# Two diffusion-transformer layers on one core: eleven local edits of order, in the opening, the attention, both FFNs and the retention

## The chip, the cores and the metric

The kernel runs on one core of a Trainium2 chip. Its engines are called PE (TensorE, matrix products; PEld is its weight load), DVE (VectorE), ACT (ScalarE), POOL (GpSimd) and SP (SyncE, which issues most transfers). The metric is device time in microseconds (us) of one execution. The kernel before took 1732.3 us (median of three runs, 1731.79 to 1732.33).

## The reference

512 latent tokens `x` and 256 context tokens `ctx`, 1024 wide, pass two layers. Layer 0 mixes by windowed grouped-query attention (16 heads of 64, 4 key heads, a sink logit), layer 1 by bidirectional retention (4 heads, 256 wide keys, 512 wide values); each is followed by a SwiGLU FFN of 2816. All products are in float32.

```python
def rms_norm(x, g):
    y = x * lax.rsqrt(jnp.mean(x * x, axis=-1, keepdims=True) + EPS)
    return y * g
def modulate(h, shift, scale):
    return h * (1 + scale) + shift
...
for i in range(DEPTH):
    mx = jnp.split(silu(c) @ ada_w[i] + ada_b[i], 6, axis=-1)        # and mc from c_ctx
    h_x = modulate(rms_norm(x, norm1_g[i]), mx[0], mx[1])            # and h_c
    out_c, out_x = (windowed_gqa_sink if i == 0 else bidir_retention)(h_x, h_c, ...)
    x = x + mx[2] * out_x
    x = x + mx[5] * swiglu(modulate(rms_norm(x, norm2_g[i]), mx[3], mx[4]), ffn_w_in[i], ffn_w_out[i])
    # the context likewise in layer 0
return x
```

The retention's decays are `log_g = log_sigmoid(decay_logit)`, eight numbers.

## The kernel before

Activations lie with the model dimension on the partitions: eight tiles of 128 x 512 for the latent tokens (`res`), four of 128 x 512 for the context (two of 256 tokens in each). A float32 product is made of three products (L148, L149, L150) in a rounded format: a weight or activation is split into a high part (a copy on ACT, `whi`) and the rest (a subtraction on DVE, `wlo`). Weights come through a ring of raw tiles (`wraw`) that SP's queue fills.

**Opening** (to about 80 us). It is written out by hand (`manual_schedule`, from L538): PE, DVE and ACT do what stands there in that order. ACT squares the eight latent tiles, DVE adds them up (`add_square`, L211), PE sums the result over the partitions with a matrix of ones (L543). `busy` (L434) is a product whose result is not used; it stands where PE would have nothing to do. `neg_half_rstd` makes of the sum the norm's factor: a logarithm, an exponential (both L101) and a square (L196) on ACT, and two operations on DVE (L197, L198). `ada_quarter` makes the first 256 shift and scale columns of the adaLN modulation: products L335, a copy of the rows (L353 for the scales, L360 for the shifts), a transpose (L355, L362), two additions (L343, L344) and the column `acol` (L114). `hidden0` applies factor and `acol` (`hs`, L449), adds the shift (ACT, L453) and makes the rest (L457). Then the first key products start (`keys`, L468).

**Attention** (80 to 300 us). Here and below a list scheduler sets each engine's order from the code's order, its dependences and its own costs. 24 blocks of queries are scored in pairs of heads (`score`: PE L756 into one of three banks `S2`, DVE L757 reads the bank, masks it and takes the minimum) and turned (transposes L776, products with values L801). A table `steps` says at which of the half blocks further work is put in: `make_q` projects the next two query heads (L148 to L150), squares them (L660), applies gain and rotation, and `norms` sums the squares (L685). `decays` at step 13 works out the retention's decay columns, 1 + 1 operations on ACT and 21 small ones on DVE (L856 to L870).

**FFN of layer 0** (300 to 865 us). `first_two` and `context_shape` make sums of tiles that stand for a two-by-two block product with seven products (`seven`, L989). The adaLN columns of layer 1 come in beside it on DVE: 48 tiles of 128 x 1024, loaded by POOL's queue into one buffer `adaw` (L269) and multiplied with the condition row (L272), once or twice each. `ada_next` takes the next of them and puts it behind the operation that it is given. `last_output` makes the FFN's last sums by halves of tokens (products into banks `pj` and `Z`, added by L1209) and the squares for the next norm.

**Retention** (865 to 1385 us). One head after the other: queries and keys (`whi` L1316, `wlo` L1317, products L1399), values, state, then the gate: `gated` multiplies norm and gate, and `values_first` starts the next head.

**FFN of layer 1** (1385 to 1728 us): `first_two` and `seven` again, with the output's sums (L254) between them.

Of the kernel before, what the change touches and what calls it, by code (L numbers as in the profile page):

```python
# [12 lines left out]
ALU = mybir.AluOpType  # L13
# [36 lines left out]
def dit_kernel(ctx, tc, xT, cT, crow, small, consts, masks, tabs0, tabs1, jtab, adaQ, adaN, adaT, wst, out):  # L50
# [272 lines left out]
    def ada_quarter_load(q):  # L323
        w = [T(st_p, 1024, "adan", 8) for _ in range(4)]
        for i in (2, 3, 0, 1):
            nc.sync.dma_start(w[i], adaQ[q, i // 2, i % 2])
        return w
# [73 lines left out]
    res0[1] = load_stream(1, 0, 4)  # L401
    wq.append(ada_quarter_load(1))
# [135 lines left out]
    with tc.manual_schedule(engines={mybir.EngineType.PE, mybir.EngineType.DVE, mybir.EngineType.Activation}):  # L538
        squares0(0, *range(KT))
        for k in range(4):  # L540
            busy(SX, k)
        tot = kvv[1]
        nc.tensor.matmul(tot, ones, ssq[0], start=True, stop=True)  # L543

        def first_fill():
# [60 lines left out]
        end = ada_unit(UNITS[1], wu[1])  # L606
        rope_key(kn[0])
        keys(1, 2)
        key_factor(0)
# [34 lines left out]
    def make_q(j, w=None, raw=None, behind=()):  # L644
# [11 lines left out]
        def shape(s):  # L656
            n = NTOK[s]
            sq, qn = t_sq(n), t_hn(n)
            nc.scalar.activation(qn, o[s], AF.Identity, scale=qk_gain[:, 0:1])
            q_done.append(nc.scalar.activation(sq, o[s], AF.Square))  # L660
# [19 lines left out]
        def norms():  # L680
            tot = pj(12)
# [169 lines left out]
    def decays(behind):  # L851

        dec = sm_t[:, C_DEC:C_DEC + 8]
        after(nc.scalar.activation(t1, dec, AF.Abs), behind)
        lnexp(t1, t1, AF.Exp, scale=-1.0)
        nc.vector.tensor_scalar(t2, t1, 2.0, None, op0=add)  # L856
        nc.vector.reciprocal(t2, t2)
        nc.vector.tensor_tensor(t1, t1, t2, op=mult)
        nc.vector.tensor_tensor(t2, t1, t1, op=mult)
        NTERM = 10  # L860
        nc.vector.tensor_scalar(t3, t2, 1.0 / (2 * NTERM + 1), None, op0=mult)
        for k in range(NTERM - 1, 0, -1):
            nc.vector.scalar_tensor_tensor(t3, t3, 1.0 / (2 * k + 1), t2, add, mult)
        nc.vector.scalar_tensor_tensor(t3, t3, 1.0, t1, add, mult)
        nc.vector.tensor_scalar(t1, dec, 0.0, None, op0=ALU.min)
        nc.vector.scalar_tensor_tensor(lg, t3, -2.0, t1, mult, add)
        nc.vector.tensor_scalar(dcol[:, 0, :], lg[:, 0:4], 128.0, None, op0=mult)
        nc.vector.tensor_scalar(dcol[:, 1, :], lg[:, 4:8], 640.0, None, op0=mult)
        nc.vector.tensor_scalar(dcol[:, 2, :], lg[:, 4:8], 384.0, None, op0=mult)
        nc.vector.tensor_scalar(dcol[:, 3, :], lg[:, 4:8], -1.0, None, op0=mult)  # L870
# [63 lines left out]
    steps.setdefault(13, []).append(lambda: decays([blocks[6].scored]))  # L934
    steps[34].append(lambda: split_o(0))
    steps[35] = [lambda: split_o(1), weight]
# [56 lines left out]
    def quarter_sums(g, u):  # L993

        l_, r_ = slice(0, 512), slice(512, 1024)
        nc.vector.tensor_tensor(g[:, l_], u[:, l_], g[:, l_], op=sub)
        nc.vector.tensor_tensor(u[:, l_], u[:, r_], u[:, l_], op=sub)
        nc.vector.tensor_tensor(u[:, r_], u[:, r_], g[:, l_], op=sub)
        nc.vector.tensor_tensor(g[:, r_], g[:, r_], u[:, r_], op=sub)  # L999
# [42 lines left out]
    def token_sums():  # L1042

        h1, h2 = THIRDS
        for k in range(4):
            t1, t2 = tm[k], tm[k + 4]
            nc.vector.tensor_tensor(t2[:, h2], t1[:, h2], t2[:, h2], op=add)
            nc.vector.tensor_tensor(t1[:, h2], t1[:, h1], t1[:, h2], op=sub)
            nc.vector.tensor_tensor(t1[:, h1], t2[:, h2], t1[:, h1], op=sub)
            nc.vector.tensor_tensor(park[:, k * 384:(k + 1) * 384], t2[:, h1], t1[:, h1], op=sub)  # L1050
# [63 lines left out]
    last_product, copies, rounded = [None], [], [None]  # L1114

    def seven(middle=None):
# [3 lines left out]
        split(g, *b11)  # L1120
# [4 lines left out]
        nc.vector.tensor_tensor(g[:, r_], g[:, r_], g[:, l_], op=sub)  # L1125
# [8 lines left out]
        if cr:  # L1134
            ada_next(half)
# [15 lines left out]
        nc.scalar.copy(c22, Y)  # L1151
# [52 lines left out]
    def last_output(acts):  # L1204
# [8 lines left out]
        for s, res, c, part in ((0, xr, HALVES[0], HALVES[0]), (1, cres, slice(SX, WIDE), slice(0, SC)),  # L1213
                                (0, xr, HALVES[1], HALVES[1])):
            for d in range(KT):
# [14 lines left out]
                sum_up(s, d, o, res, part, s == 1 or c.start == 0)  # L1230
                if s and d == 2:
# [14 lines left out]
    ada_q = []  # L1246
# [13 lines left out]
    for gsz in FFN_GROUPS:  # L1260
        acts = []
        for i in range(gsz):
# [4 lines left out]
            else:  # L1267
                a, end = seven(last_sum if f == PLAIN else None)
                acts.append(a)
                if f == PLAIN:  # L1270
                    ends.pop(0)()
                    cr = cond_rows(fp)
                if i or f == PLAIN + 2:
                    ada_next(end)
# [4 lines left out]
    assert not ada_q  # L1279
# [188 lines left out]
    for hd in range(RH):  # L1468
# [74 lines left out]
        for e, o in halves(Y2):  # L1543
            nc.vector.tensor_tensor(qt[e][:, HALVES[0]], qt[e][:, HALVES[0]], o, op=add)
# [10 lines left out]
        for i in range(2):  # L1555
# [4 lines left out]
            nc.vector.tensor_tensor(v11[i], g12[i], v11[i], op=add)  # L1560
            w2.append(split_chunk(v11[i]))
        parted = last_split[:]
        w3 = [split_chunk(g12[0])]
# [137 lines left out]
        product_v(Zg, quarter_of(4), w22, False, (1,))  # L1701
        for t in range(2):
# [337 lines left out]
```

## Time and profile before

| | |
|---|---|
| median of three runs | 1732.3 us (1731.79 to 1732.33) |
| the profiled execution | 1730.06 us, span 1728.3 us, granted clock 0.999 |
| PE busy | 1706.5 us, 99% of the span |
| DVE, ACT, POOL busy | 1336.0, 841.4 and 120.9 us |
| bytes read from HBM | 201.75 MB, 118 GB/s over the span |

A row of the timeline gives the start in us from the first instruction, the length, the engine, the line of the kernel, the operation, output and input tiles with their shapes, and in brackets the idle time before it with what ended it. A row of the waits gives the engine and line that waited, what for, the us in total, how often, and the longest. A row of a stretch gives its ends and length, the busy time and count of PE, PEld, DVE, ACT and POOL, then PE's granted clock, the share of the transfer engines and GB/s.

### The profile page before, as it was taken

The page shows a single profiled execution, that of the slowest core. Times are in us where ns is not written, and L with a number is a line of the kernel's source. Part 1 is how long each engine was busy: PE and PEld are TensorE (multiplying, and loading weights), DVE is VectorE, ACT ScalarE, POOL GpSimd, SP SyncE. Part 2 cuts the span into 40 slices and gives each one's busy share as a digit, 9 for nine tenths or more (in the row PEclk, how much of TensorE's full clock was granted, in tenths as well). Part 3 has the DMA queues.
Part 4 walks back from the last instruction along what each step waited for, and adds up shares of the span by engine and source line. Part 5 has one row for each costly group of instructions (what it writes and reads, how often), then busy time and mean ns, then how long its engine had stood idle before and what let it go on. Part 6 is the DMA issues. An engine that isn't in the chain of part 4 may idle for free.

```text
span 1728.3 us, 28150 instructions
## 1 busy us (share of the span) xinstructions
PE 1706.5 (99%) x11090; PEld 1535.7 (89%) x11090; DVE 1336.0 (77%) x2377; ACT 841.4 (49%) x1509; POOL 120.9 (7%) x266
## 2 busy tenths in 40 slices
PE   8999999999999999999999999999999999999999
PEld 5888887899999999999998798898898999999998
DVE  6888696488778777787899858758768898778774
ACT  5667696264434233342565624524525555445442
POOL 0033443000000000000000000000000100000000
PEclk9999999999999999999999999999999999999999
DMA  9500014233243434343423534433433333233322
GB/s 374 226 26 26 13 58 163 74 122 111 95 136 129 141 111 158 110 147 110 147 100 122 183 99 131 160 110 118 157 106 112 98 98 122 74 122 99 107 77 86
DMA packets 61908, 205.67 MB, mean 119 GB/s; under 512 B 6864, under 2 KB 7760, under 8 KB 61648
## 3 DMA queue, kind: packets, MB, share of 16 engines
q1 hardware_dynamic: 54864, 178.71, 30.6%
q0 software_dynamic: 6912, 25.17, 4.5%
q8 instruction: 87, 1.43, 0.3%
q14 instruction: 45, 0.37, 0.1%
HBM read 201.75 MB, written 2.10 MB: 118 GB/s over the span
## 4 chain that ended last, share of the span: by engine, by line
PE 40%; DVE 7%; DMA 2%; ACT 1%; issue 1%; SPq 0%; ACTq 0%; DVEq 0%
PE Y L989 6%; PE Z L1399 6%; PE Y L1386 3%; PE Z L989 3%; PE pj L148 2%; PE pj L150 2%; PE pj L149 2%; PE pj L1399 2%; PE X L1386 1%; PE X L989 1%; DMA wraw<-in_wst_dram 1%; DVE wlo L1317 1%; PE X L1399 1%; PE X L148 1%; PE X L150 1%
## 5 line engine op out<-in xcount | busy, mean ns | idle before, releaser
L989 PE MATMUL Y<-aq,whi 128*128 128x384 f32 x640 | 173.7, 335 | 1.1 <-ACT hn L1140 0.7
L254 DVE SCALAR_TENSOR_TENSOR res<-pj,mod,res 128x512 f32<-128x512 f32 (+1 forms) x102 | 74.5, 731 | 68.7 <-PE pj L150 68.3
L989 PEld LDWEIGHTS Y<-aq,whi 128*128 128x128 f32 x640 | 116.6, 188 | 2.1 <-ACT hn L1140 1.4
L140 ACT CAST whi<-wraw 128x1024 fp32r<-128x1024 f32 x75 | 78.7, 1049 | 72.1 <-DMA wraw<-in_wst_dram 25.2
L141 DVE TENSOR_TENSOR wlo<-wraw,whi 128x1024 fp32r<-128x1024 f32 x75 | 91.7, 1223 | 28.5 <-ACT whi L140 27.7
L989 PE MATMUL Y<-aq,wlo 128*128 128x384 f32 x320 | 107.2, 335 | 0.5 <-DVE wlo L166 0.4
L272 DVE CUSTOM_DVE_ANT_0 y<-adaw,crow,small_sb 128x1024 bf16<-128x1024 f32 x64 | 81.9, 1280 | 23.1 <-DMA adaw<-in_adaT_dram 23.1
L1316 ACT CAST whi<-wraw 128x1024 fp32r<-128x1024 f32 x55 | 57.6, 1049 | 72.3 <-PE Y L150 52.3
L101 ACT ACTIVATE pr<-pr,stat,qs 128x513 f32<-128x513 f32 (+2 forms) x96 | 74.1, 775 | 19.1 <-DVE stat L763 17.7
L1399 PE MATMUL Z<-whi,sA 128*128 128x512 f32 x256 | 80.7, 391 | 0.6 <-ACT whi L1316 0.6
L1317 DVE TENSOR_TENSOR wlo<-wraw,whi 128x1024 fp32r<-128x1024 f32 x55 | 67.0, 1223 | 16.4 <-ACT whi L1316 16.3
L165 ACT CAST whi<-wraw 128x1024 fp32r<-128x1024 f32 x40 | 42.0, 1051 | 73.8 <-PE Z L150 43.3
L770 POOL TENSOR_SCALAR pr<-pr,stat 128x512 f32<-128x512 f32 (+2 forms) x96 | 66.5, 706 | 86.5 <-DVE stat L767 67.4
L148 PE MATMUL pj<-ax,whi 128*128 128x512 f32 x176 | 68.9, 392 | 0.7 <-DVE res L254 0.7
L150 PE MATMUL pj<-ax,whi 128*128 128x512 f32 x176 | 68.7, 390 | 0.0
L149 PE MATMUL pj<-ax,wlo 128*128 128x512 f32 x176 | 68.6, 389 | 0.0
L269 POOL DMA_DIRECT2D adaw<-in_adaT_dram x48 | 25.6, 533 | 512.6 <-DVE mod L272 420.7
L989 PEld LDWEIGHTS Y<-aq,wlo 128*128 128x128 f32 x320 | 60.1, 188 | 1.1 <-DVE wlo L166 1.1
L757 DVE CUSTOM_DVE_ANT_0 pr<-S,mask,qs 128x256 f32<-128x256 f32 (+1 forms) x96 | 52.7, 567 | 10.7 <-PE S L756 8.5
L148 PE MATMUL pj<-act,whi 128*128 128x512 f32 (+1 forms) x156 | 60.1, 385 | 0.6 <-DVE res L1209 0.6
L989 PE MATMUL Y<-sA,whi 128*128 128x256 f32 x304 | 60.1, 280 | 0.2 <-ACT res L1842 0.2
L1835 ACT CAST whi<-wraw 128x1024 fp32r<-128x1024 f32 x38 | 39.2, 1052 | 43.1 <-DVE wraw L999 21.6
(620 smaller groups left out, 5613.2 us busy)
## 6 DMA issues: line engine op xcount, KB each, us to landing
wraw<-in_wst_dram SPq DMA_DIRECT2D x231, 512.0 KB, 3.6
adaw<-in_adaT_dram POOLq DMA_DIRECT2D x48, 512.0 KB, 3.8
wx<-in_wst_dram SPq DMA_DIRECT2D x28, 512.0 KB, 4.4
adan<-in_adaQ_dram SPq DMA_DIRECT2D x16, 512.0 KB, 7.3
adan<-in_adaN_dram SPq DMA_DIRECT2D x16, 512.0 KB, 8.0
res<-in_xT_dram SPq DMA_DIRECT2D x16, 256.0 KB, 5.4
q<-in_adaN_dram SPq DMA_DIRECT2D x16, 256.0 KB, 3.7
aq<-in_adaN_dram SPq DMA_DIRECT2D x12, 256.0 KB, 5.3
```

Source lines behind the costliest of these rows:

```text
L101: ins = nc.scalar.activation(*args, **kw)
L140: after(nc.scalar.copy(hi, raw), behind)
L141: after(nc.vector.tensor_tensor(lo, raw, hi, op=sub), low)
L148: after(nc.tensor.matmul(o, whi, xhi, start=first, stop=False), behind)
L149: nc.tensor.matmul(o, wlo, xhi, start=False, stop=False)
L150: return nc.tensor.matmul(o, whi, xlo, start=False, stop=last)
L254: return nc.vector.scalar_tensor_tensor(res[d], o, mods[l, s][:, part, d:d + 1], res[d], mult, add)
L272: after(nc.vector.tensor_tensor_reduce(junk, w, cr[:, s * 1024:(s + 1) * 1024], 1.0, sm_t[:, C_ADAB + l * 48 + j:C_ADAB + l * 48 + j + 1], ...
L989: ins = nc.tensor.matmul(o, p, r, start=first and k + i == 0, stop=k == 3 and i == 2, skip_group_check=not first)
L1317: last_split[0] = nc.vector.tensor_tensor(lo, raw, hi, op=sub)
L1386: ins = nc.tensor.matmul(o[:, e * SC:(e + 1) * SC], p[:, ws], r, start=first and k + e + i == 0, stop=k == 3 and i == 2, skip_group_check= ...
L1399: ins = nc.tensor.matmul(o, p, r, start=first and k + i == 0, stop=k == 3 and i == 2, skip_group_check=not first)
```

## The change

Eleven edits, in the order of the program:

1. Opening: the squares of the seventh latent tile are no longer added by DVE; PE adds them into the sum by a product of its own. Sum and factor are made in two halves of 256 tokens, each step for both halves. Six `busy` products instead of four stand ahead of it. The factor is emitted ahead of `ada_quarter` and no longer between its two products. The shift columns come behind the second `hs` instead of the first.
2. Two context transfers go out between the second and third transfer of the second adaLN quarter instead of ahead of it.
3. The second adaLN unit's products stand behind `keys(1, 2)`.
4. `make_q`: for context queries the square goes ahead of the gain copy; the first head pair's sums go into the bank `pO`.
5. `decays`: one operation per step from step 12 on, instead of all at step 13.
6. `context_shape`: ACT adds the shift to latent columns 384 to 512 only; the sums of tiles add it for columns 0 to 384.
7. `seven` of layer 0: from the second group on the copy of a weight waits for the last copy of the group before.
8. The adaLN tiles of layer 1 in other places: one in the weight's preparation, one behind each adaLN end, the rest in `last_output` behind its second sum.
9. Retention, first head: the last query sums behind the first split of values, and the splits behind the second sum.
10. Retention, end of heads 1 to 3: the gate's additions with the next value weights' splits between them, then `values_first`, then the four `gated`.
11. FFN of layer 1: the order of weight copies, sums and products is tied to the copy of the first product and to the multiplication of the group before.

```diff
-        squares0(0, *range(KT))
-        for k in range(4):
+        opening_sq = lambda n: T(st_p, 512, "hs", 3)[:, :n]
+        for k in range(KT - 2):
+            add_square(0, k, res0[0][k], tmp=opening_sq)
             busy(SX, k)
-        tot = kvv[1]
-        nc.tensor.matmul(tot, ones, ssq[0], start=True, stop=True)
+        y0, z0, tail = ssq[0], t_sq(SX), [opening_sq(SX) for _ in range(2)]
+        tot = [t[:, 0:SC] for t in kvv[0:2]]
+        nc.scalar.activation(tail[0], res0[0][KT - 2], AF.Square)
+        for o, c in zip(tot, HALVES):
+            nc.tensor.matmul(o, ones, tail[0][:, c], start=True, stop=False)
+        for o, c in zip(tot, HALVES):
+            nc.scalar.activation(tail[1][:, c], res0[0][KT - 1][:, c], AF.Square)
+            nc.vector.tensor_tensor(y0[:, c], y0[:, c], tail[1][:, c], op=add)
+            nc.tensor.matmul(o, ones, y0[:, c], start=False, stop=True)
...
+        for step in range(4):
+            for o, c in zip(tot, HALVES):
+                first_factor(step, o, c)
...
-        c0, c1 = ada_quarter(0, wq[0], nc.vector.tensor_copy, lambda: None, first_fill,
-                             lambda: neg_half_rstd(ssq[0], t_sq(SX), tot, D))
+        c0, c1 = ada_quarter(0, wq[0], nc.vector.tensor_copy, lambda: None, first_fill)
         busy(SX)
-        hidden0(0, 0, 1, between=(lambda: low(0, quarters[0]), lambda: low(1, quarters[0])), shifts=c0)
+        hidden0(0, 0, 1, between=(lambda: low(0, quarters[0]), lambda: low(1, quarters[0])), shifts=c0, at=1)
...
-            tot = pj(12)
+            tot = pj(12) if j else pO()[:, 0:12]
...
-    steps.setdefault(13, []).append(lambda: decays([blocks[6].scored]))
+    for i, op in enumerate(decays()):
+        steps.setdefault(12 + i, []).append(lambda i=i, op=op: after(op(), [blocks[12 + i >> 1].scored]))
...
-            for s, c in ((0, slice(0, SX)), (1, slice(SX, WIDE))):
+            for s, c in ((0, slice(384, SX)), (1, slice(SX, WIDE))):
...
+        if waiting:
+            waiting.clear()
+            ada_next(last)
...
-        if cr:
-            ada_next(half)
...
+                while ada_q and not s and d == 1:
+                    ada_next(added[1])
...
+        for ins in [] if hd else late:
+            after(ins, parted)
...
-        gated(2)
-        gated(3)
         if last:
+            gated(2)
+            gated(3)
...
-            b11, Yv, vt, ins = values_first(first_weights_v(hd + 1))
+            b11, Yv, vt, ins = values_first(next_v)
+            for n in (2, 3, 0, 1):
+                gated(n)
...
-        split(u[:, 512:1024], *b22)
-        quarter_sums(g, u)
+        after(nc.scalar.copy(b22[0], u[:, 512:1024]), p1s if f == 5 else [])
+        nc.vector.tensor_tensor(b22[1], u[:, 512:1024], b22[0], op=sub)
+        sums = quarter_sums(g, u)
+        if added:
+            after(sums[0], muls[-1:])
+            after(sums[1], added[:1])
```

How the edits move instructions is seen at three places. The rows name line, operation, output and input tiles, width, and a count of equal rows; lines are those of each kernel. The first is DVE in the opening, from the additions of squares (`y_245`) to the first two modulated tiles (`hs`). Before:

```order
L211 TENSOR_TENSOR y_245<-y_245,sq 128x512 x7
L353 COPY rows<-pT 128x128
L343 TENSOR_TENSOR mod_74<-pT,small_sb 128x2
L344 TENSOR_TENSOR mod_74<-pT,mod_74 128x2
L114 SCALAR_TENSOR_TENSOR acol_78<-mod_74,gm_85 128x2
L197 SCALAR_TENSOR_TENSOR sq<-kvv,sq 128x512
L198 SCALAR_TENSOR_TENSOR y_245<-sq,y_245 128x512
L449 SCALAR_TENSOR_TENSOR hs<-res,acol_78,y_245 128x512
L343 TENSOR_TENSOR mod_74<-pT,small_sb 128x2
L344 TENSOR_TENSOR mod_74<-pT,mod_74 128x2
L449 SCALAR_TENSOR_TENSOR hs<-res,acol_78,y_245 128x512
```

The same stretch of DVE after the change (L562 and L563 are the factor's two operations, L355 the copy of the scale rows, L345 and L346 the additions of columns, L450 the modulated tile):

```order
L211 TENSOR_TENSOR y_245<-y_245,hs 128x512 x5
L551 TENSOR_TENSOR y_245<-y_245,hs 128x256 x2
L562 SCALAR_TENSOR_TENSOR sq<-kvv,sq 128x256
L563 SCALAR_TENSOR_TENSOR y_245<-sq,y_245 128x256
L562 SCALAR_TENSOR_TENSOR sq<-kvv,sq 128x256
L563 SCALAR_TENSOR_TENSOR y_245<-sq,y_245 128x256
L355 COPY rows<-pT 128x128
L345 TENSOR_TENSOR mod_74<-pT,small_sb 128x2
L346 TENSOR_TENSOR mod_74<-pT,mod_74 128x2
L114 SCALAR_TENSOR_TENSOR acol_78<-mod_74,gm_85 128x2
L450 SCALAR_TENSOR_TENSOR hs<-res,acol_78,y_245 128x512 x2
```

The copy of the scale rows with its additions and `acol` stood ahead of the factor's operations and now stands behind them, and both `hs` now stand ahead of the shift's additions. The second place is PE at the start, from the `busy` products to the transpose of the scale rows. Before:

```order
L434 MATMUL kvv<-res,ones_sb 128x512 x4
L543 MATMUL kvv<-y_245,ones_sb 128x512
L335 MATMUL pT<-adan,ccol 32x128 x16
L355 MATMUL pT<-const_sb,rows 128x128
L335 MATMUL pT<-adan,ccol 32x128 x16
```

The same stretch of PE after the change (L548 adds the seventh tile's squares, L552 the other ones'):

```order
L435 MATMUL kvv<-res,ones_sb 128x512 x6
L548 MATMUL kvv<-hs,ones_sb 128x256 x2
L552 MATMUL kvv<-y_245,ones_sb 128x256 x2
L337 MATMUL pT<-adan,ccol 32x128 x16
L357 MATMUL pT<-const_sb,rows 128x128
L337 MATMUL pT<-adan,ccol 32x128 x16
```

Two more `busy` products and four half-width products stand where one full-width product stood. The third place is PE in the attention around 165 us of the trace before, behind the query heads' sums of squares: scores (`S_...`, one name for each bank turn), transposes (`pT`) and query projections (`pj`). Before:

```order
L756 MATMUL S_2259<-kc,q 128x256 x2
L756 MATMUL S_2263<-k,q 128x384 x2
L756 MATMUL S_2269<-kc,q 128x256 x2
L776 MATMUL pT<-const_sb,pr 128x128 x8
L756 MATMUL S_2273<-k,q 128x384
L685 MATMUL pj<-const_sb,sq 128x2 x2
L756 MATMUL S_2273<-k,q 128x384
L148 MATMUL pj<-h,whi 128x512
L756 MATMUL S_2300<-kc,q 128x256 x2
```

The same stretch of PE after the change (L783 are the scores, L803 the transposes, L712 the sums of squares); it ends with the second projection product of eleven that stand ahead of the next score product, `S_2265`:

```order
L783 MATMUL S_2251<-kc,q 128x256 x2
L783 MATMUL S_2255<-k,q 128x384 x2
L803 MATMUL pT<-const_sb,pr 128x128 x3
L783 MATMUL S_2261<-kc,q 128x256 x2
L803 MATMUL pT<-const_sb,pr 128x128 x5
L712 MATMUL pj<-const_sb,sq 128x2 x2
L148 MATMUL pj<-h,whi 128x512
L149 MATMUL pj<-h,wlo 128x512
```

The fourth score of the group came right behind the transposes; now eleven projection products stand between the transposes and it.

More of the change, by code (lines that the diff above doesn't have):

```diff
@@ L658, in shape @@
             sq, qn = t_sq(n), t_hn(n)
+            square = lambda: q_done.append(nc.scalar.activation(sq, o[s], AF.Square))
+            if s:
+                square()
             nc.scalar.activation(qn, o[s], AF.Identity, scale=qk_gain[:, 0:1])
-            q_done.append(nc.scalar.activation(sq, o[s], AF.Square))
+            if not s:
+                square()
             sqs.append(sq)
@@ L1119, in seven @@
         b11 = w_parts(fp, 1)
-        split(g, *b11)
+        after(nc.scalar.copy(b11[0], g), copied_up if f == PLAIN + 1 else [])
+        nc.vector.tensor_tensor(b11[1], g, b11[0], op=sub)
         t1 = T(fp, 512, "bhi", 1, F32R), T(fp, 512, "blo", 1, F32R)
@@ L1150, in seven @@
         product(Y, operand[3], b3, 0, False)
-        nc.scalar.copy(c22, Y)
+        copied_up[:] = [nc.scalar.copy(c22, Y)]
         nc.vector.tensor_tensor(c22, c22, c21, op=add)
@@ L1841, in seven @@
         product(Y, operand_a("11"), b11, 0, True)
-        nc.scalar.copy(p1, Y)
+        p1s[:] = [nc.scalar.copy(p1, Y)]
         product(Z, operand_a(1), b14, 0, True)
```

93 lines of the change are left out of this document (53 added, 40 removed).

## The prediction

> **What bounds the kernel now.** I read the busy times first, then the waits of TensorE (PE), then busy time by stretch, then single rows where PE stands. The busy times say which engine a microsecond has to be taken from (the second line is a group of transfers: issuer, count, size, us from issue to landing; it is needed further below):
>
> ```profile
> PE 1706.5 (99%) x11090; PEld 1535.7 (89%) x11090; DVE 1336.0 (77%) x2377; ACT 841.4 (49%) x1509; POOL 120.9 (7%) x266
> ...
> adaw<-in_adaT_dram POOLq DMA_DIRECT2D x48, 512.0 KB, 3.8
> ```
>
> The span is 1728.3 us and PE is busy for 1706.5 of it. The diff leaves PE's products as they are, so all that it can win is PE's idle time, some 22 us, and time at a lower clock. The waits of PE (engine, line, what it waited for, us in total, times, longest) name the idle time:
>
> ```profile
> PE kvv L434 <- DMA res<-in_xT_dram: 4.1, 1, 4.1
> PE S L756 <- DVE stat L757: 2.8, 2, 2.2
> PE kvv L543 <- DVE y L211: 1.8, 1, 1.8
> PE pj L468 <- ACT h L453: 1.6, 2, 1.0
> PE Y L989 <- ACT hn L1140: 0.7, 1, 0.7
> PE pj L148 <- DVE res L254: 0.7, 1, 0.7
> PE Z L1399 <- ACT whi L1316: 0.6, 1, 0.6
> PE Z L1399 <- DVE wlo L1317: 0.6, 1, 0.6
> PE pj L148 <- DVE res L1209: 0.6, 1, 0.6
> PE pj L685 <- ACT sq L660: 0.5, 1, 0.5
> PE Y L989 <- DVE wlo L166: 0.4, 1, 0.4
> PE X L148 <- ACT sq L107: 0.4, 1, 0.4
> PE Y L989 <- ACT sq L1151: 0.4, 1, 0.4
> PE pj L148 <- DVE qs L688: 0.3, 1, 0.3
> ```
>
> The first row is the wait for the first input and no edit touches it. Nearly every other row has an edit of its own in the diff, so the change is a list of small repairs, each worth at most its row. The stretches (length, PE, PEld, DVE, ACT, POOL busy, granted clock, DMA share, GB/s) show where nothing is left:
>
> ```profile
> 157.00:165.00 8.00, 6.00 (x49) 5.50 (x48) 7.84 (x20) 5.88 (x12) 2.29 (x4) 1.00 0.09 20
> 165.00:172.00 7.00, 6.75 (x34) 5.78 (x35) 6.69 (x25) 3.57 (x11) 2.04 (x4) 0.76 0.14 53
> 1000.00:1380.00 380.00, 379.88 (x2096) 331.33 (x2095) 282.72 (x397) 168.95 (x257) 4.40 (x9) 1.00 0.37 122
> ```
>
> From 1000 to 1380 us PE idles 0.12 us: heads 2 to 4 of the retention have nothing to give. The stretch 165 to 172 is the only one after the start with a clock below 1.00.
>
> **Decays (steps 12 to 35).** The rows around the longest wait (start, length, engine, line, operation, in brackets the idle time before it):
>
> ```profile
> 149.62 0.17 DVE L856 TENSOR_SCALAR lg_t<-lg_t 128x8 f32<-128x8 f32 x1
> ...
> 156.13 0.16 DVE L870 TENSOR_SCALAR dcol<-lg 128x4 f32<-128x4 f32 x1
> ...
> 162.02 1.21 DVE L141 TENSOR_TENSOR wlo<-wraw,whi 128x1024 fp32r<-128x1024 f32 x1
> ...
> 163.27 0.68 DVE L675 TENSOR_TENSOR q<-hn,q 64x512 fp32r<-64x512 f32 x1
> ...
> 165.25 0.45 PE L756 MATMUL S<-k,q 128*128 128x384 f32 x1 [2.25 <-DVE stat L757]
> ```
>
> VectorE (DVE) runs 21 such small operations from 149.62 to 156.13, about 21 x 0.17 = 3.6 us, and from 157 to 165 it is busy 7.84 of 8 us: it is behind, and PE waits 2.25 us for a score bank that it has not read. Right after that the clock is at 0.76 of full speed over 7 us, which costs 7 x 0.24 = 1.7 us. Spread over 24 steps, at most three or four of the 21 stand ahead of that point, so DVE arrives some 3 us earlier, more than the wait. The new PE order speaks for it too: eleven products of 512 columns stand ahead of the score product that waited, where there were none. I take the whole: **-3.9** (2.2 + 1.7). Bounds: 0, if another late DVE operation takes the place, and -4.5 with the second wait of that row (2.8 in all).
>
> [...]
>
> **Other waits, with one answer each.** The attention queries (square before the gain copy, the first sum in another bank): rows 0.5 and 0.3; two scalar operations swap, nothing is added; **-0.6**, between 0 and -0.8. The first part of the FFN (the shift no longer added by ACT over 384 latent columns; c22's copy ahead of the next weight's): rows 0.4 (L107) and 0.4 (L1151); ACT loses eight operations, DVE adds twelve with a scalar in place of plain ones, hidden by DVE's idle time (it is busy 77% of the span); **-0.7**, between +0.3 and -0.8. The adaLN tiles of layer 1 (DVE) in other places: rows 0.7 (L1140) and 0.4 (L166); **-0.9**, between +0.5 and -1.1. First retention head: rows 0.6 (L1316) and 0.6 (L1317); **-1.0**, between 0 and -1.2. In the later heads the gate's additions and next splits now stand ahead of the norm's multiplies, but `values_first` of the next head keeps PE busy behind them; nothing. FFN of layer 1: row 0.7 (L254); **-0.7**, between 0 and -0.8.
>
> **Last output of layer 0's FFN.** The rows there before:
>
> ```profile
> 848.79 1.28 DVE L272 CUSTOM_DVE_ANT_0 y<-adaw,crow,small_sb 128x1024 bf16<-128x1024 f32 x1 [0.92 <-DMA adaw<-in_adaT_dram]
> 850.01 0.48 DVE L1209 SCALAR_TENSOR_TENSOR res<-pj,mod,res 128x256 f32<-128x256 f32 x1
> 850.40 1.27 DVE L272 CUSTOM_DVE_ANT_0 y<-adaw,crow,small_sb 128x1024 bf16<-128x1024 f32 x1
> ...
> 850.88 0.28 PE L150 MATMUL pj<-act,whi 128*128 128x256 f32 x1
> 851.00 0.28 PE L148 MATMUL pj<-act,whi 128*128 128x256 f32 x1
> ```
>
> One tile's two products stood here, the second behind the first sum. Now the first sums come sooner, but one tile more falls in this stage, and there is one buffer: the last tile's transfer of 3.8 us starts when the tile before it has been read. Four sums stand between them, each of which PE takes 12 products at 0.12 us from start to start, about 1.4 us, to feed, so the transfer mostly lies beside 5.6 us of PE's work. The 0.6 may go, or come back three sums later: **0**, between -0.6 and +2.0 (two products more of 1.28 on DVE, less what the banks cover).
>
> **The opening.** This is the one step that I expect to lose. Rows before:
>
> ```profile
> 4.08 6.70 PE L434 MATMUL kvv<-res,ones_sb 128*128 128x512 f32 x8 [4.08 <-DMA res<-in_xT_dram]
> 9.42 3.08 DVE L211 TENSOR_TENSOR y<-y,sq 128x512 f32<-128x512 f32 x4 [0.35 <-ACT sq L210]
> 12.55 1.12 PE L543 MATMUL kvv<-y,ones_sb 128*128 128x512 f32 x2 [1.77 <-DVE y L211]
> 14.76 0.29 DVE L353 COPY rows<-pT 128x128 f32<-128x128 f32 x1 [2.26 <-PE pT L335]
> 15.86 0.16 DVE L114 SCALAR_TENSOR_TENSOR acol<-mod,gm 128x2 f32<-128x2 f32 x1
> 16.57 0.70 PE L434 MATMUL kvv<-res,ones_sb 128*128 128x256 f32 x2
> 16.66 0.69 DVE L198 SCALAR_TENSOR_TENSOR y<-sq,y 128x512 f32<-128x512 f32 x1
> 17.39 0.75 DVE L449 SCALAR_TENSOR_TENSOR hs<-res,acol,y 128x512 f32<-128x512 f32 x1
> 19.21 0.74 PE L468 MATMUL pj<-h,whi 128*128 128x512 f32 x2 [0.97 <-ACT h L453]
> ```
>
> The path to the first key product is squares, sum, factor, modulated input. PE was late by 1.77 us for the sum (12.55), since DVE added squares until 12.50. Now two more products of 512 that only keep PE busy stand ahead of it. An instruction of such a product shows as two rows (four as 8): 4 more rows, at 0.84 (6.70 / 8) or, warm, 0.56 (1.12 / 2). They end at about 4.08 + 6.70 + 2.2 = 13.0, or 12.3 if the warm pitch comes a little earlier. Behind them stand four products of 256 columns, 8 rows of 0.35 (0.70 / 2): the first half's sum ends at 12.3 + 6 x 0.35 = 14.4, the second's at 15.1, where the whole sum ended at 13.67. DVE's shorter chain is so lost behind PE. ACT and DVE then work in halves, which overlap: behind the sum the factor took 17.35 - 13.67 = 3.7 us, and by halves some 3.0 from the second sum, about 18.1 to 18.4, **+0.8 to +1.1**.
>
> Then the order on DVE: the copy of the scale rows (L353) with the transpose, two additions and `acol` behind it took 14.76 to 16.02 and lay beside ACT's work on the factor. They now stand behind all four factor operations, so that their 1.26 us come after y: the first `hs` starts at 18.2 + 1.3 = 19.5 where it was 17.39, **+2.1**. The shift columns now wait for the second `hs` as well, **+0.75**. First keys at 19.21 + 2.85, about 22.1: **+2.9**. PE has from there no slack until 80 us. Bounds: +1.4 (half factors quicker, shift columns no later) and +4.5 (PE idles some 2.6 us for the late copy, and the 2.25 us gap above was followed by a window at half speed, 1.7). The context rows' later loads (needed after the first keys, which move too) and the second unit behind `keys(1, 2)`: nothing, they are covered by PE's products.
>
> **Sum.** -3.9 - 0.6 - 0.7 - 0.9 - 1.0 - 0.7 + 0 + 2.9 = -4.9. The profiled execution took 1730.06 (span 1728.3 and 1.8 around it), 2.2 below the median of 1732.3; against the median the sum gives **1727.4**. About 0.2%, 3.5 us, is what a measurement of this kernel tells from no change: 1728.8 to 1735.8 is "same".
>
> **Rivals.**
> - The opening gains as its halves suggest: if PE's clock is up earlier and DVE's copy finds its rows while it waits anyway, the 1.8 us wait of L543 goes and the order costs nothing: 1732.3 - 7.8 - 1.8 = 1722.7. For it: DVE's additions are shorter by a whole row. Against it: DVE runs in order, and its new order has the copy last. Chance 0.10.
> - The freed DVE time is given back in the attention stage: the score bank's wait appears at another query group. 1727.4 + 3.9 = 1731.3. For it: DVE's run of a weight split (1.2 us) and four query operations without reading a score is still there at each query group. Chance 0.20.
> - The small repairs bring new waits of the same size, so that only decays and opening count: 1732.3 - 3.9 + 2.9 = 1731.3. For it: these are 0.2 to 0.7 us each, and every one is a swap in an order. Chance 0.15.
> - Slower, by one mechanism in the attention stage: the new scheduling makes score waits as long as the one at 165.25 at three places. Each costs 2.2 + 1.7 (the clock falls after it): 1731.3 + 2 x 3.9 = 1739.1 with the decays' gain lost and two beside it. It decides from the point where PE has less ready work than DVE's run lasts, 1.2 + 4 x 0.5 + 0.7 = 3.9 us (L141; four like L675, two of them half as wide; a copy); PE's new order has eleven products of 512 columns and some transposes there, at twice the 0.12 us of the 256-column rows above about 3 us. So the margin is thin; it is slower than before from the second such place (1735.2). Chance 0.10.
>
> **How the numbers follow.** My forecast has 0.45. It lies 1.4 us within "faster" and its terms scatter by 2 to 3 us, so 0.30 of the 0.45 is faster and 0.15 same; the first rival is all faster (0.10); the second and third (0.35) are same but for 0.08, which is faster, and 0.02 slower; the slower rival adds 0.10, of which 0.04 stays within 0.2%. Faster 0.48, same 0.44, slower 0.08. With the bounds of the opening and of the last output, the range goes from 1721.5 (the first rival) to 1735 (the second mishap in the attention).
>
> **What the profile after will show.** Decays: no PE wait above 1 us at 150 to 180 us and no stretch below clock 1.00. Opening: the first key product near 22, the scale rows' copy behind both factor halves, PE idle about 2.6 us ahead of it. The waits of L1140, L166, L1316, L1317, L254 and L107 gone from PE's list. I am wrong if the first keys start before 20 us, if a score wait of over 2 us stands elsewhere, or if PE waits at 845 to 860 us by more than 1 us.

## The result, and the profile after

The changed kernel took 1755.79 us (median of four runs, 1753.18 to 1758.21) against 1732.05 for the kernel before on the same chip: 1.0139 times the time, with a 95% interval of 1.0122 to 1.0157. It is 24 us slower; the forecast was 5 us faster, and no rival priced it so high. The profiled execution took 1753.18, its span is 1751.4 us. The line of busy times:

```profile
PE 1714.3 (98%) x11100; PEld 1540.1 (88%) x11100; DVE 1333.6 (76%) x2379; ACT 839.2 (48%) x1513; POOL 122.8 (7%) x266
```

DVE and ACT do no more work than before (1336.0 and 841.4 us), so the time is not work that was added. PE idles 37.1 us of the span (21.8 before), and its products are busy 7.8 us longer. The waits of PE in the changed kernel:

```profile
PE Y L1011 <- DVE wlo L166: 9.1, 8, 2.3
PE kvv L435 <- DMA res<-in_xT_dram: 4.2, 1, 4.2
PE pT L357 <- DVE rows L355: 2.4, 1, 2.4
PE pj L150 <- DVE act L1095: 2.1, 1, 2.1
PE pj L148 <- ACT act L1094: 1.6, 1, 1.6
PE X L1428 <- DVE wlo L1346: 1.4, 2, 1.1
PE Y L1415 <- DVE wlo L1346: 1.3, 1, 1.3
PE Y L1011 <- ACT res L1884: 1.3, 1, 1.3
...
PE pT L932 <- DMA q<-in_adaN_dram: 1.1, 1, 1.1
...
PE pj L149 <- DVE wlo L141: 0.9, 1, 0.9
```

The waits for the scores at 165 us, for the queries (L685) and for L254 are gone or short. A new one leads the list: the seven-product stage (L1011, before L989) waits eight times for the low part of a weight (`wlo`, L166), 9.1 us in all. Marks in the two traces say where the 23 us of span come from. The first key product starts at 21.20 (before 19.21), the last score of the attention at 298.47 (297.81), the group of seven products that resumes at 522.98 before resumes at 522.67; then the same marks of the next groups are at 621.02 (614.68), 717.64 (706.77) and 812.93 (800.34), and the first retention product at 900.66 (880.78). So most of the loss, 20 us, lies between 523 and 900 us, in the FFN of layer 0: there PE idles 16.1 us (2.0 before), and its granted clock is 0.99 (1.00 before). Another 2.5 us stand behind it, at 900 to 1000 us, where PE's waits sum to 3.9 us (1.4 before). Two stretches there (490 to 530 is an output stage, 530 to 590 the seven-product stage behind it), before:

```profile
490.00:530.00 40.00, 40.00 (x232) 36.15 (x231) 29.68 (x45) 9.37 (x13) 2.11 (x4) 1.00 0.37 120
530.00:590.00 60.00, 60.00 (x347) 58.96 (x346) 49.08 (x74) 25.54 (x43) 3.70 (x7) 1.00 0.46 148
```

and after:

```profile
490.00:530.00 40.00, 40.00 (x233) 36.19 (x232) 23.29 (x35) 8.43 (x11) 0.00 (x0) 1.00 0.21 66
530.00:590.00 60.00, 55.73 (x306) 54.41 (x305) 49.86 (x77) 25.65 (x43) 5.28 (x10) 0.97 0.47 153
```

In the output stage DVE has lost 6.4 us of work (29.68 to 23.29) and POOL issues no transfer, and in the stage behind it PE idles 4.3 us of 60, at a clock of 0.97. What went missing are the adaLN tiles. DVE's waits at 500 to 870 us for their transfers, before and after:

```profile
DVE y L272 <- DMA adaw<-in_adaT_dram: 18.8, 12, 3.8
```

```profile
DVE y L272 <- DMA adaw<-in_adaT_dram: 35.9, 34, 3.6
```

Twelve waits have become 34. DVE's order shows why; here T is a product of an adaLN tile (L272) and o a sum of the output stage (L254), from the first product on, before and after:

```
before  TTTTTToooToToooTooooTooooToTTTTTTTTTToooTooooTo
after   TTTTTTooooooooooooooooTTTTTTTTTTTTTTToooooooooo
```

Before, five products (of four tiles) stood between the sums of an output stage, where DVE waits for PE anyway (8.6 us of the 40 at 490 to 530 us, for products of L150). Now none does, and some fourteen products stand in one run in the seven-product stage. The rows of DVE around the first output stage of the changed kernel:

```profile
486.57 1.28 DVE L272 CUSTOM_DVE_ANT_0 y<-adaw,crow,small_sb 128x1024 bf16<-128x1024 f32 x1 [3.64 <-DMA adaw<-in_adaT_dram]
...
525.88 0.56 DVE L1095 TENSOR_TENSOR act<-sq,act 128x384 fp32r<-128x384 f32 x1 [2.52 <-ACT act L1094]
526.36 1.28 DVE L272 CUSTOM_DVE_ANT_0 y<-adaw,crow,small_sb 128x1024 bf16<-128x1024 f32 x1
...
572.24 1.29 DVE L272 CUSTOM_DVE_ANT_0 y<-adaw,crow,small_sb 128x1024 bf16<-128x1024 f32 x1 [1.29 <-DMA adaw<-in_adaT_dram]
...
574.39 1.22 DVE L166 TENSOR_TENSOR wlo<-wraw,whi 128x1024 fp32r<-128x1024 f32 x1
```

No tile for 40 us, then one right behind L1095, which is the `end` of the group's first seven products (the last operation that `seven` returns; the "adaLN end" of the change's list is this one). Edit 8 ties a tile to that `end`, and in the code it stands ahead of `output(prev)`. PE does the output stage before those products are finished. There is one buffer `adaw`, and it is given out in the order of the code: the tile that waits for the late `end` holds it, and the output's own four tiles queue behind. POOL's rows show the buffer held: it issues a transfer at 488.16, and the next one 42 us later, released by DVE's product:

```profile
488.16 0.53 POOL L269 DMA_DIRECT2D adaw<-in_adaT_dram  x1 [6.00 <-DVE mod L272]
530.28 0.53 POOL L269 DMA_DIRECT2D adaw<-in_adaT_dram  x1 [41.59 <-DVE mod L272]
```

In the kernel before it issues four in that time. Here the four tiles come when the stage that had room for them is over. At 572.24 the second effect shows: DVE stands 1.29 us for a transfer, and the split of the next weight (574.39) stands behind it in DVE's queue. PE gets that weight 2.35 us late:

```profile
575.66 0.45 PE L1011 MATMUL Y<-aq,wlo 128*128 128x384 f32 x1 [2.35 <-DVE wlo L166]
```

### The profile page after: what moved, and what is told of

Read it like the earlier page. It is cut to its first block, busy times and chain, and to the rows that moved or that the text cites. A ratio compares the mean times of both kernels' runs of the same rounds, so it can differ in the third digit from the quotient of the medians.

```text
span 1751.4 us, 28141 instructions
## 1 busy us (share of the span) xinstructions
PE 1714.3 (98%) x11100; PEld 1540.1 (88%) x11100; DVE 1333.6 (76%) x2379; ACT 839.2 (48%) x1513; POOL 122.8 (7%) x266
## 4 chain that ended last, share of the span: by engine, by line
PE 41%; DVE 6%; DMA 1%; ACT 1%; issue 1%; POOL 0%; ACTq 0%; DVEq 0%; SPq 0%
PE Z L1428 6%; PE Y L1011 6%; PE Y L1415 3%; PE Z L1011 3%; PE pj L148 2%; PE pj L150 2%; PE pj L149 2%; PE pj L1428 2%; PE X L1415 1%; PE X L1011 1%; DMA wraw<-in_wst_dram 1%; PE X L150 1%; PE X L1428 1%; PE Y L149 1%; PE X L149 1%; PE Y L150 1%
## 5 line engine op out<-in xcount | busy, mean ns | idle before, releaser
L1011 PE MATMUL Y<-aq,whi 128*128 128x384 f32 x640 | 174.2, 336 | 2.5 <-ACT hn L1173 1.2
L254 DVE SCALAR_TENSOR_TENSOR res<-pj,mod,res 128x512 f32<-128x512 f32 (+1 forms) x102 | 74.4, 730 | 64.4 <-PE pj L150 64.2
L1011 PEld LDWEIGHTS Y<-aq,whi 128*128 128x128 f32 x640 | 116.9, 188 | 3.9 <-ACT hn L1166 1.6
L1011 PE MATMUL Y<-aq,wlo 128*128 128x384 f32 x320 | 108.2, 338 | 9.7 <-DVE wlo L166 9.1
L272 DVE CUSTOM_DVE_ANT_0 y<-adaw,crow,small_sb 128x1024 bf16<-128x1024 f32 x64 | 82.1, 1283 | 40.4 <-DMA adaw<-in_adaT_dram 40.4
L140 ACT CAST whi<-wraw 128x1024 fp32r<-128x1024 f32 x75 | 78.6, 1048 | 70.7 <-PE Z L150 24.7
L1345 ACT CAST whi<-wraw 128x1024 fp32r<-128x1024 f32 x55 | 57.5, 1050 | 75.6 <-PE Y L150 52.9
L1011 PEld LDWEIGHTS Y<-aq,wlo 128*128 128x128 f32 x320 | 60.2, 188 | 12.5 <-DVE wlo L166 11.6
L150 PE MATMUL pj<-ax,whi 128*128 128x512 f32 x176 | 68.7, 390 | 0.0
L1011 PE MATMUL Y<-sA,whi 128*128 128x256 f32 x304 | 60.0, 280 | 1.3 <-ACT res L1884 1.3
L149 PE MATMUL pj<-act,wlo 128*128 128x512 f32 (+1 forms) x156 | 60.1, 385 | 0.9 <-DVE wlo L141 0.9
L1877 ACT CAST whi<-wraw 128x1024 fp32r<-128x1024 f32 x38 | 39.3, 1052 | 44.8 <-DVE wraw L1021 23.6
L148 PE MATMUL pj<-act,whi 128*128 128x512 f32 (+1 forms) x156 | 60.1, 385 | 0.0
L150 PE MATMUL pj<-act,whi 128*128 128x512 f32 (+1 forms) x156 | 59.5, 382 | 0.0
```

Source lines behind the costliest of these rows:

```text
L140: after(nc.scalar.copy(hi, raw), behind)
L148: after(nc.tensor.matmul(o, whi, xhi, start=first, stop=False), behind)
L149: nc.tensor.matmul(o, wlo, xhi, start=False, stop=False)
L150: return nc.tensor.matmul(o, whi, xlo, start=False, stop=last)
L254: return nc.vector.scalar_tensor_tensor(res[d], o, mods[l, s][:, part, d:d + 1], res[d], mult, add)
L272: after(nc.vector.tensor_tensor_reduce(junk, w, cr[:, s * 1024:(s + 1) * 1024], 1.0, sm_t[:, C_ADAB + l * 48 + j:C_ADAB + l * 48 + j + 1], ...
```

## Experiments

The kernel before ran beside them on the same chips: 1730.68 us in the first four, 1730.86 in the next, 1730.09 in the last. Ratios are to it, with their 95% interval; as it moved by up to 2 us between sessions (1732.05 beside the changed kernel), runs of different sessions are compared by their ratios.

**All but edit 8.** Its lines are put back to those of before.

```diff
-        if waiting:
-            waiting.clear()
-            ada_next(last)
...
+        if cr:
+            ada_next(half)
...
-                while ada_q and not s and d == 1:
-                    ada_next(added[1])
...
-                if f > PLAIN:
-                    ada_next(end)
-                if i or f == PLAIN + 2:
-                    waiting.append(f)
+                if i or f == PLAIN + 2:
+                    ada_next(end)
```

> All edits but the adaLN tiles' (edit 8 undone). From the traces the changed kernel loses 20 us between the first group of seven products and the first retention product (-0.3 us at 523 us, +19.9 at 900 us). If edit 8 is the whole of that: 1755.8 - 20 = 1736, so 3 to 4 us above the kernel before, from the opening (+2), the first retention head and the last FFN. If the loss comes from the other edits in this stage (the shift's place, the copy tied to the group before): still about 1755.

Measured: 1729.04 us, ratio 0.9992 (0.9983 to 1.0002). Edit 8 is the whole loss: 1.0139 less 0.9992 is 25 us (27 between the medians). The 1736 that I expected was too high, as I counted only the 20 us up to the first retention product; the waits behind it go as well (at 900 to 1000 us 1.6 us are left of 3.9). The other ten edits together make no difference that this measurement shows.

**Edit 8 alone** on the kernel before, the same lines the other way round.

> The kernel before with edit 8 alone. If edit 8 makes the loss by itself: 1732 + 18 to 20 = 1750 to 1752. If it needs the other edits (a DVE that they already make late): under 1740.

Measured: 1756.06, ratio 1.015 (1.0134 to 1.0165). It makes the loss by itself, 25 us, some 4 us more than I expected; nothing else in the change is needed for it.

**Which part of edit 8.** First, the tile at the group's first `end` is moved into the preparation of the next weight, all else as changed:

```diff
-                if f > PLAIN:
-                    ada_next(end)
                 if i or f == PLAIN + 2:
+                    ada_next(end)
+                if f > PLAIN:
                     waiting.append(f)
```

> The changed kernel, but the tile that stands behind the first adaLN end of each group goes into the next weight's preparation instead; eleven tiles a group as before, and the place ahead of the weight's split is kept (and used once more). Theory 1: that one tile holds the only buffer until the group's first end, which comes after the output stage, so that the output's four tiles come late and fourteen products stand back to back behind 4 us transfers, ahead of weight splits; without it 1736 to 1738. Theory 2: a product ahead of the split b24 delays that split by itself; then 1752 to 1758, as there is one more of them.

Measured: 1728.6, ratio 0.9993 (0.9984 to 1.0002). One tile for each group, tied to another instruction, takes the whole loss away (theory 1, again some 8 us below its number). In its trace the stretch behind the output stage has PE at 60.00 of 60 us again, and of PE's waits at 500 to 900 us two short ones are left:

```profile
490.00:530.00 40.00, 40.00 (x233) 36.14 (x232) 30.10 (x46) 9.53 (x13) 2.11 (x4) 1.00 0.40 124
530.00:590.00 60.00, 60.00 (x347) 58.91 (x346) 49.05 (x74) 25.95 (x43) 3.70 (x7) 1.00 0.44 146
```

```profile
PE Y L1011 <- ACT hn L1166: 0.6, 1, 0.6
PE Y L1011 <- DVE wlo L166: 0.4, 1, 0.4
```

Then the other half of the edit: the tile in the preparation goes behind the split again, the first `end` keeps its tile.

```diff
-        if waiting:
-            waiting.clear()
-            ada_next(last)
         b24 = w_parts(fp, 1)
...
         nc.vector.tensor_tensor(b3[1], u, b3[0], op=sub)
+        if waiting:
+            waiting.clear()
+            ada_next(half)
```

> The other half: the first end of a group keeps its tile, but the product in the preparation stands behind the split b24 again, as before the change. Theory 1: 1752 to 1756, nothing won, since the tiles still fall back to back. Theory 2: 1737 to 1740.

Measured: 1751.58, ratio 1.0122 (1.0107 to 1.0137), 3 us under the whole change by the ratios, whose intervals overlap, and slightly below what theory 1 gave. The rival mechanism (a product ahead of a split) is so at most a small part, and only while the tiles come in a run: in the run before, with the product ahead of the split at more places, it cost nothing that shows. A second buffer for the tiles, which would take the hold away and leave the places, was not tried.

**Transfer or products.** Is it the wait for transfers that makes DVE late, or the products' own time? The transfers of 47 tiles are left out; each product is held behind the one before, so that the order of T and o stays that of the change.

```diff
-            w = T(room, 1024, "adaw", 1 if l else 3)
-        (nc.gpsimd if l else nc.sync).dma_start(w, adaT[l, j])
+            w = (held[:1] or [T(room, 1024, "adaw", 1 if l else 3)])[0]
+        if not held:
+            (nc.gpsimd if l else nc.sync).dma_start(w, adaT[l, j])
```

> The changed kernel with all products of the adaLN tiles of layer 1 in their places and order (each held behind the one before), but only the first of the 48 tiles is loaded and all products use it: 47 transfers of 512 KB are left out. Theory (the loss is DVE standing ahead of weight splits until a transfer into the single buffer lands): DVE's waits for these transfers (35.9 us at 500 to 870 us) go, and the loss with them, 1733 to 1738. Rival (fourteen products of 1.28 us in one stretch are too much work for DVE beside the splits, whatever the transfers do): 1748 or more.

Measured: 1743.26, ratio 1.0073 (1.0058 to 1.0088), between the two. By the ratios some 11 us of the 25 are gone and 14 remain; PE idles 10.3 us at 500 to 900 us, where it was 16.1 in the changed kernel and 0.8 without edit 8. Without waits for transfers the postponed products all become due at the end of the output stage, and run closely:

```profile
527.13 1.28 DVE L277 CUSTOM_DVE_ANT_0 y<-adaw,crow,small_sb 128x1024 bf16<-128x1024 f32 x1
...
529.47 1.28 DVE L277 CUSTOM_DVE_ANT_0 y<-adaw,crow,small_sb 128x1024 bf16<-128x1024 f32 x1
...
531.14 1.28 DVE L277 CUSTOM_DVE_ANT_0 y<-adaw,crow,small_sb 128x1024 bf16<-128x1024 f32 x1
```

and PE at 500 to 900 us waits for the splits that stand behind them (the second row is ACT's copy of a weight, late by the same chain: at 544.32 us ACT has waited 2.33 us for a sum of DVE):

```profile
PE Z L1019 <- DVE blo L166: 3.7, 3, 1.2
PE Y L1019 <- ACT whi L165: 3.1, 4, 1.8
```

So my theory had the cause right (the postponed tiles) and only half of the way: both the transfers and the products' own 1.28 us make DVE late once they come in a run.

**The opening.** On top of edit 8 undone, the halves (edit 1) are undone as well.

> Edit 8 and the opening's halves (edit 1) undone, all else as changed. Theory (the scale rows' copy behind the factor delays the start): the first key product goes from 20.3 to about 19.1 us and the time falls by 1.2 to 2.0 from 1729.0, to 1727.0 to 1727.8. Rival (the delay is made up behind it, or the halves gain as much): within 0.5 of 1729.0.

Measured: 1728.23, ratio 0.9981 (0.9972 to 0.9991); first key product at 18.95 us, where it was 20.32 with the halves. Then the halves are kept, with the factor handed back to `ada_quarter`, where it stands behind the scale rows' copy, and the shift columns behind the first `hs`:

```diff
-        c0, c1 = ada_quarter(0, wq[0], nc.vector.tensor_copy, lambda: None, first_fill)
+        c0, c1 = ada_quarter(0, wq[0], nc.vector.tensor_copy, lambda: None, first_fill, factor)
```

> Edit 8 undone; the sum and the factor in halves are kept, but the factor is worked out where it stood before the change, behind the copy of the scale rows with its transpose and columns, and the shift columns stand behind the first modulated tile again. Theory (only DVE's order is at fault, the halves are a gain of some 0.9 us for the factor): first key product at 18.2 to 18.9 us, 1726.5 to 1727.5. Rival (the two busy products and the four half products on PE are at fault): first key product still after 20 us, 1729.

Measured: 1729.1, ratio 0.9985 (0.9976 to 0.9995). Both times lie above what the theory gave, and the time can't tell these three kernels apart; the trace can. In the kernel before PE waited 0.4 us for the copy of the scale rows:

```profile
PE pT L355 <- DVE rows L353: 0.4, 1, 0.4
```

In the changed kernel, where the copy stands behind the factor on DVE, it waits 2.38:

```profile
17.76 0.33 PE L357 MATMUL pT<-const_sb,rows 128*128 128x128 f32 x1 [2.38 <-DVE rows L355]
...
21.20 0.73 PE L469 MATMUL pj<-h,whi 128*128 128x512 f32 x2 [0.50 <-ACT h L454]
```

With the copy ahead of it:

```profile
14.07 0.29 DVE L355 COPY rows<-pT 128x128 f32<-128x128 f32 x1 [2.54 <-PE pT L337]
...
16.49 0.43 DVE L563 SCALAR_TENSOR_TENSOR y<-sq,y 128x256 f32<-128x256 f32 x1
```

the first key product starts at 18.78. So DVE's order is at fault, and not the products on PE, which this run keeps: with the factor ahead of the copy the first key product starts at 20.3 to 21.2 us in all eight profiles, otherwise at 18.8 to 19.6 in all six. The halves by themselves show neither gain nor loss. The factor is ready at 16.92 here, but at 17.69 in the fastest version below, whose opening is the same; without halves it is ready at 17.35 (the kernel before) and 17.09 (the halves undone).

**The decays.** Edit 5 alone on the kernel before, then edits 5 and 8 undone in the changed one.

> The kernel before with edit 5 (decays) alone. By the forecast's term the 2.2 us wait at 165 us and the half-speed window behind it go: 1730.7 - 3.9 = 1726.8. Rival, by the trace of the changed kernel, whose attention stage is only 0.3 us shorter: the time is given back at later waits (scores turned by POOL, a transfer of adaLN weights at 269 us): 1729.5 to 1730.7.

Measured: 1728.58, ratio 0.9987 (0.9977 to 0.9996): some 2 us (0.7 to 4), between forecast and rival.

> Edits 5 and 8 undone, all else as changed. If the decays' spreading is worth 3.9 beside the other edits: 1729.0 + 3.9 = 1732.9, with the wait at 165 us back. If it is given back: 1729 to 1730.

Measured: 1725.44, ratio 0.9964 (0.9951 to 0.9977). That is neither expectation: beside the other edits the kernel is faster without the spreading, by 3.6 us between the medians and 4.8 by the ratios, whose intervals don't overlap. The wait that it removes at 165 us is back in this kernel, 1.78 us long:

```profile
165.88 0.62 PE L783 MATMUL S<-k,q 128*128 128x384 f32 x2 [1.78 <-DVE stat L784]
```

but the kernel with the spreading (edit 8 undone) has a wait at 269 us instead, for the transfer of half an adaLN unit, which is not among the waits of the kernel before:

```profile
269.26 0.43 PE L932 MATMUL pT<-q,ccol 128*32 128x128 f32 x8 [1.99 <-DMA q<-in_adaN_dram]
```

All nine profiles that have the spreading beside the other edits show this wait, 1.1 us or more; the two without it have a wait for such a transfer of 0.7 and 0.8 us. So the gain is given back. Why the kernel is even slower with the spreading stays open: PE's waits at 150 to 300 us sum to 3.1 us with it and 3.4 without. A part is the clock: over 255 to 285 us it was 0.94 in the profile with the spreading, which is 1.8 us of the 30, and 1.00 in the one without. That the transfer's buffer (a tile of `q`) comes free no earlier when PE does is my reading; it wasn't tried.

**Retention and the FFN of layer 1.** Edits 8, 9 and 10 undone, then 8 and 11.

> Edits 8, 9 and 10 undone. By the forecast's term the retention's edits are worth 1.0: 1729.0 + 1.0 = 1730.0. By the traces, in which PE's waits at 900 to 1000 us sum to the same with and without them (2.4 and 2.6 us): 1729.0.

Measured: 1729.76, ratio 0.9999 (0.9989 to 1.0008), not told apart from 1729.04. PE's waits at 900 to 1000 us are 2.1 us without edits 9 and 10 (0.7, 0.6, 0.6, 0.2), 1.6 with them.

> Edits 8 and 11 undone. By the forecast's term edit 11 is worth 0.7: 1729.7. By the trace the wait for the sum of layer 1's FFN is gone but a wait of 1.2 us for the first product's copy stands at 1458 us instead: 1728.5.

Measured: 1728.78, ratio 0.999 (0.9981 to 0.9999), the same as with edit 11. From 1380 us on PE has one wait in either kernel, with edit 11:

```profile
PE Y L1011 <- ACT res L1880: 1.1, 1, 1.1
```

and without it:

```profile
PE pj L148 <- DVE res L254: 0.6, 1, 0.6
```

One wait has been changed for another.

**The fastest version**: edits 5 and 8 undone, the opening in halves with the copy first.

> Edits 5 and 8 undone, and the opening's halves with the scale rows' copy ahead of the factor. Sum of the two runs: 1725.4 (edits 5 and 8 undone) less the 1.5 us that the first key products come earlier: 1723.9. If the earlier start is given back behind it, as the times of the runs on the opening alone leave open: 1725.4.

Measured: 1724.71, ratio 0.9968 (0.9955 to 0.998): faster than both kernels, by 0.3% against before, and not to be told from the version without the opening's repair (1725.44).

## Why the prediction was wrong, point by point

- **The adaLN tiles, the step that failed: "-0.9, between +0.5 and -1.1".** They cost 25 us, alone and beside the others, and the two waits that were to go, 0.7 and 0.4 us, became 1.0 and 9.1. I looked at the two waits that the edit aimed at, and at the one tile more in the last output, where I did see the single buffer and the products behind it. So the term had only the waits that the edit removes, and put at next to nothing what the moved tiles do to the ones behind them. I did not follow the order of all 48 tiles: the order on DVE before and after shows, without any time, that no tile was left in the output stages. What the runs showed in its place: the tile at the first `end` holds the one buffer for 42 us, fourteen products then run in one row ahead of the weight splits, and PE waits for these. The mechanism was at hand (a product that waits, splits behind it, PE behind them); its place and its size were missed. No rival had it: mine for slower was in the attention stage.
- **Decays, -3.9.** The wait at 165 us went as forecast, but alone the edit is worth 2.3, and beside the other edits a wait at 269 us takes its place and the kernel is 4 to 5 us slower with the edit than without it, not all of which the waits explain. My second rival ("given back in the attention stage") was right in kind, at a transfer and not at a score. The 1.7 us at the lower clock (0.76 over 165 to 172 us in the kernel before) were no fixed part of the wait (below).
- **Opening, +2.9.** Right in sign and mechanism: the copy behind the factor, 2.4 us of idle PE ahead of it (forecast 2.6). The first keys came at 21.20, 2.0 later (forecast 22.1); with edit 8 undone they came at 20.32, 1.4 later than without the halves. The factor was mis-sized: it ended at 17.51, 0.16 later than before (with edit 8 undone at 16.48), where I had +0.8 to +1.1, as I gave the four half-width products 0.35 us a row and they followed each other at 0.22. In time it cost 0.8 us between the medians, 1.9 by the ratios, within the measurement. PE's granted clock is 1.00 over 0 to 20 us in the kernel before and in the changed one, so neither trace shows a clock that comes up earlier, as my first rival would have it.
- **Retention, -1.0, and FFN of layer 1, -0.7.** Half a microsecond of waits, and nothing: the waits named went, others came. That was my third rival.
- **Attention queries, -0.6, and the FFN's first part, -0.7.** The queries' two waits are not among the changed kernel's, and the first score comes 1.0 us later than before where the first keys come 2.0 later. In the first part of the FFN two waits of 0.4 and 0.3 us are left of three (0.4, 0.4, 0.2); no run takes it apart.
- **Last output, 0.** The wait of 0.6 (L1209) is gone in the profile with edit 8 undone, but 0.5 and 0.7 us long in two others that have the same code there. In the changed kernel two waits of 1.6 and 2.1 us stand ahead of it (L1094, L1095), with the stage now at 863 us and later: the third sign of being wrong, a wait of over 1 us in this stage, came true.
- **Smaller slips.** ACT does not lose eight operations in the FFN's first part, it does the same eight on 128 columns in place of 512. The diff does not leave PE's products quite as they are, as the opening adds some. The list of waits leaves out the row of 0.4 us for the scale rows, the one that edit 1 made 2.4. The range's lower end, 1721.5, lies 1.2 below the rival that it is taken from (1722.7).
- **Without the failed term** my sum gives -4.0; the kernel without edit 8 is at -1.6, not told from no change.

## What to carry to other kernels

Where work comes through one buffer in the order of the code, one piece tied to a late instruction holds back all pieces behind it (here for 42 us): look at the order of the whole row of pieces, not at the place of the piece that was moved. Work that fills the idle time of an engine costs nothing only in the stage that has the idle time; moved by 40 us, as here, it stood ahead of work that another engine waited for, and the time rose by 25 us. A stall of a few tenths removed by a swap in an order is often paid for by another swap: without the failed term this list was priced at -4.0 and came to -1.6, which can't be told from nothing.

## What the runs showed of the hardware

The same wait was not always followed by a lower clock of PE. In the kernel before 2.25 us of idle PE at 165 us were followed by a clock of 0.76 over 7 us (0.50 from 167.5 to 170.5 us); with edit 8 alone, where the code up to there is the same, 2.19 us were not:

```profile
165.31 0.45 PE L756 MATMUL S<-k,q 128*128 128x384 f32 x1 [2.19 <-DVE stat L757]
```

```profile
165.00:172.00 7.00, 6.54 (x38) 5.33 (x39) 6.69 (x26) 4.58 (x14) 2.35 (x6) 1.00 0.14 53
```

The fastest version had 1.85 us of idle PE there and 0.76 again:

```profile
165.00:172.00 7.00, 7.00 (x33) 6.24 (x34) 6.87 (x26) 4.56 (x12) 2.81 (x7) 0.76 0.10 39
```

So a wait of 1.85 us was followed by a lower clock and one of 2.19 us was not. The wait at 269 us shows the same in nine profiles. In four of them the clock was lower (over 255 to 285 us 0.94 three times and 0.89 once), with waits of 1.3 to 2.0 us; in the other five it was 1.00, with waits of 1.1 to 2.4 us. The shortest wait of those with the lower clock (the run without loads, PE idle 2.1 us of the 30) and the longest of the others (the retention's edits undone, PE idle 3.2 us):

```profile
255.00:285.00 30.00, 27.95 (x248) 20.39 (x247) 19.03 (x71) 18.24 (x46) 11.86 (x28) 0.94 0.74 255
255.00:285.00 30.00, 26.84 (x252) 20.55 (x252) 19.37 (x73) 18.10 (x45) 12.21 (x28) 1.00 0.75 255
```

What lowered the clock in one profile and not in the next, no run shows. A loss of 1.7 us behind a wait of about 2 us should have been a chance in my sum and not a term.
